# Residual rows scaled and shifted by a norm's vectors 900 instructions behind the norm instead of 400

## The chip, the cores and the metric

The kernel runs on one core of one Trainium2 chip. The metric is the device time of one execution in microseconds (us). A core has five engines with queues of their own: TensorE (PE, with its weight loads shown apart as PEld), VectorE (DVE), ScalarE (ACT), GpSimd (POOL) and SyncE (SP), which here only issues transfers. Each engine takes its instructions strictly in the order in which the program has them; engines wait for each other through semaphores.

## The reference, cut to what matters

One layer of a decoder over 512 tokens of 1024 values: three sublayers, each followed by a layer norm of `ALPHA * h + f(h)`.

```python
def layer_norm(x, g, b):
    mu = jnp.mean(xf, axis=-1, keepdims=True)
    var = jnp.mean(jnp.square(xf - mu), axis=-1, keepdims=True)
    return ((xf - mu) * lax.rsqrt(var + LN_EPS) * g + b).astype(x.dtype)

h = layer_norm(x, ln_in_g, ln_in_b)
f = hybrid_mixer(h, ...)                       # three kinds of attention, one output projection w_out
h = layer_norm(ALPHA * h + f, ln_mix_g, ln_mix_b)
f = mem_attn(h, mem, w_mem_q, w_mem_kv, w_mem_o)
h = layer_norm(ALPHA * h + f, ln_mem_g, ln_mem_b)
f = sq_relu_mlp(h, w_up, b_up, w_down, b_down)
h = layer_norm(ALPHA * h + f, ln_ffn_g, ln_ffn_b)
```

The norm's result is used twice: at once, as the next sublayer's input, and much later, times ALPHA, as the residual that the next sublayer's output is added to.

## The kernel before

Tokens lie in four tiles of 128 rows, `res[0]` to `res[3]` (128 x 1024, float32), which hold the residual. Matrix products run in three passes on a high and a low part of each operand (names `h_...` and `l_...`; `mm3` writes the three). A weight block is loaded by SP (`r_...`), its high part is a cast, its low part a subtraction (`split`).

A norm works like this. The last product of a sublayer (`gemm_tok`, banks `ps_wo` for the mixer and `ps_wmo` for the memory attention) finishes token tile by token tile. For each tile `residual` adds two PSUM banks to `res[t]` and takes statistics (`st_...`, `mv_...`, `ve_...`), all on DVE; POOL computes the reciprocal root (`rs_...`), and `center` on DVE subtracts the mean and multiplies by `rs`. For each pair of tiles TensorE then transposes the centred rows (`ps_lt`); ACT or DVE applies the norm's two vectors along partitions (`h32`), and a cast and a subtraction split it into the next sublayer's operand (`h1T0` to `h1T7` after the mixer, `h2T0` to `h2T7` after the memory attention). With those the next products start: `ps_q` (queries of the memory attention, `w_mem_q`) and `ps_up` (the MLP's first product, `w_up`), first on the columns of tokens 0 to 255, then on the rest.

The residual needs the same scale and shift along rows. `gb_rows` loads the two vectors, broadcast to 128 rows and multiplied by ALPHA (`gbc_mix`, `bbc_mix`, later `gbc_mem`, `bbc_mem`), and `gain_shift` multiplies `res[t]` by the one and adds the other: two operations of 128 x 1024 for each tile, eight for a norm, on DVE or on POOL (`any_tt` leaves the engine open). Their result is read by the adds of the next sublayer's end, over 70 us later for the mixer's norm and some 200 us later for the memory norm.

The order on each engine is not the order of the source. Every instruction is recorded with a due number (`clock`, one more for each instruction), and `issue` lays all of them out with a cost for each: at each step it takes, over all engines, the instruction that can start first by its own clock, among those with equal start the one with the lower due number. It looks no further ahead than 560 due numbers (`LOOK`) beyond the oldest instruction that is not yet placed. `either` instructions go to the engine on which they would end first. `gain_shift` raises the due number of its two instructions by `later`:

```python
def gain_shift(hat, gb, t, later=0.0):
    nc.clock += later
    any_tt(hat[t], hat[t], gb[0], OP.mult)
    any_tt(hat[t], hat[t], gb[1], OP.add)
    nc.clock -= later
```

It is called with `GAIN_LATER` behind the mixer's norm and behind the memory norm. The norm of the input calls it with no delay. At 400 the eight operations lie within the 560 that `issue` looks ahead when their rows are ready.

Of the kernel before, what the change touches and what calls it, by code (L numbers as in the profile page):

```python
# [364 lines left out]
def trunk_kernel(ctx: ExitStack, tc: tile.TileContext, x, mem, ln_in_g, ln_in_b, w_in, gate_w2,  # L365
# [764 lines left out]
# [5 lines that stand above are left out]
# [19 lines left out]
    for t in range(NT):  # L1154
        gain_shift(res, gb, t, GAIN_LATER)

# [51 lines left out]
    for t in range(NT):  # L1208
        gain_shift(res, gb, t, GAIN_LATER)

# [176 lines left out]
GATE_AHEAD = 80.0  # L1387
LOOK = 560.0
KV_STEPS = (0, 0, 0, 1, 3, 3, 2, 4, 1, 1)
GAIN_LATER = 400.0  # L1390
W_SLACK = 300.0
M_SLACK = 600.0
DOWN_LATER = 60.0
# [23 lines left out]
```

## Time and profile before

| | us |
|---|---|
| median of 3 runs | 826.19 (826.02 to 827.07) |
| the profiled execution | 825.4 |
| its span in the trace | 823.6 |
| TensorE busy in the span | 792.5 (96%) |
| DVE busy | 631.3 (77%) |
| ACT busy | 329.2 (40%) |
| POOL busy | 158.2 (19%) |

Times in the trace count from the span's start. Mean granted clock of TensorE over the span is 0.99 of full speed. The mixer's last product ends at 350.0 us, the memory attention runs until 475.8 us, the MLP from there to the end. The two norms concerned therefore lie around 335 to 370 us and 460 to 495 us.

### The profile page before, as it was taken

The page shows a single profiled execution, that of the slowest core. Times are in us where ns is not written, and L with a number is a line of the kernel's source. Part 1 is how long each engine was busy: PE and PEld are TensorE (multiplying, and loading weights), DVE is VectorE, ACT ScalarE, POOL GpSimd, SP SyncE. Part 2 cuts the span into 40 slices and gives each one's busy share as a digit, 9 for nine tenths or more (in the row PEclk, how much of TensorE's full clock was granted, in tenths as well). Part 3 has the DMA queues.
Part 4 walks back from the last instruction along what each step waited for, and adds up shares of the span by engine and source line. Part 5 has one row for each costly group of instructions (what it writes and reads, how often), then busy time and mean ns, then how long its engine had stood idle before and what let it go on. Part 6 is the DMA issues. An engine that isn't in the chain of part 4 may idle for free.

```text
span 823.6 us, 11289 instructions
## 1 busy us (share of the span) xinstructions
PE 792.5 (96%) x4177; PEld 662.8 (80%) x4177; DVE 631.3 (77%) x1111; ACT 329.2 (40%) x634; POOL 158.2 (19%) x173
## 2 busy tenths in 40 slices
PE   7999999999999899989999989999999999899995
PEld 5997769777877888888878889888888888678884
DVE  7737999997649983886553799767777776798778
ACT  4506634577535540233330143333323232585420
POOL 5320142354622210227340210000000000110001
PEclk9999999999999999999999999999999999999998
DMA  8520331603244534023322024645546555467532
GB/s 239 137 53 15 100 94 27 179 9 103 75 152 159 165 120 150 27 77 103 114 92 77 26 77 142 217 154 186 197 137 214 196 174 175 138 219 240 196 126 103
DMA packets 99927, 106.70 MB, mean 130 GB/s; under 512 B 10448, under 2 KB 79136, under 8 KB 99872
## 3 DMA queue, kind: packets, MB, share of 16 engines
q1 hardware_dynamic: 97344, 99.00, 38.1%
q10 hardware_dynamic: 2528, 6.98, 2.5%
q8 instruction: 33, 0.54, 0.3%
q14 instruction: 22, 0.18, 0.1%
HBM read 94.69 MB, written 10.49 MB: 128 GB/s over the span
## 4 chain that ended last, share of the span: by engine, by line
PE 68%; DVE 16%; issue 2%; ACT 1%; DMA 1%; POOL 0%; DVEq 0%; ACTq 0%; POOLq 0%
PE ps_up L356 20%; PE ps_dn L356 17%; PE ps_wmo L356 4%; PE ps_wo L356 4%; PE ps_q L356 3%; DVE res L356 2%; PE ps_km L356 2%; PE ps_z L356 2%; DVE acc L356 2%; PE ps_vm L356 2%; PE ps_gg L356 1%; PE ps_dq L356 1%; PE ps_mo L356 1%; DVE m L356 1%; DVE s L356 1%
## 5 line engine op out<-in xcount | busy, mean ns | idle before, releaser
L356 PE MATMUL ps_up<-h2T,h_up 128*128 128x512 f32 (+1 forms) x576 | 161.1, 366 | 0.0
L356 PEld LDWEIGHTS ps_up<-h2T,h_up 128*128 128x128 f32 x576 | 104.0, 189 | 17.6 <-DVE h2T L356 0.2
L356 PE MATMUL ps_up<-h2T,l_up 128*128 128x512 f32 (+1 forms) x288 | 104.8, 366 | 0.5 <-DVE l_up L356 0.5
L356 ACT ACTIVATE ur<-ps_up,gb_all 128x512 f32<-128x512 f32 x32 | 22.1, 690 | 108.7 <-PE ps_up L356 108.7
L356 PEld LDWEIGHTS ps_up<-h2T,l_up 128*128 128x128 f32 x288 | 54.1, 189 | 9.5 <-DVE l_up L356 0.7
L356 PE MATMUL ps_dn<-h_dn,a 128*128 128x512 f32 x192 | 59.3, 389 | 0.0
L356 DVE TENSOR_TENSOR l_dn<-r_dn,h_dn 128x1024 fp32r<-128x1024 f32 (+1 forms) x44 | 45.2, 1026 | 5.1 <-ACT h_dn L356 3.7
L356 PE MATMUL ps_dn<-h_dn,ends 128*128 128x512 f32 x128 | 47.7, 396 | 0.7 <-DVE ends L356 0.7
L356 POOL TENSOR_TENSOR a<-keep,a 128x1024 fp32r<-128x1024 f32 x1 | 4.1, 4067 | 228.3 <-PE ps_dn L356 228.3
L356 PE MATMUL ps_q<-h1T,h_wmq 128*128 128x256 f32 (+1 forms) x192 | 45.7, 329 | 0.0
L356 ACT ACTIVATE h<-ps_lt,gb_all 128x256 f32<-128x256 f32 x20 | 10.2, 566 | 85.6 <-PE ps_lt L356 84.8
L356 PEld LDWEIGHTS ps_dn<-h_dn,a 128*128 128x128 f32 x192 | 36.0, 188 | 7.5
L356 PE MATMUL ps_wmo<-h_wmo,oT 128*128 128x512 f32 x128 | 40.7, 393 | 0.0
L356 DVE TENSOR_TENSOR l_up<-r_up,h_up 128x1024 fp32r<-128x1024 f32 x32 | 38.9, 1220 | 2.2 <-ACT h_up L356 0.5
L356 PE MATMUL ps_wo<-h_wo,mix 128*128 128x512 f32 x128 | 40.3, 392 | 0.0
L356 PE MATMUL ps_dn<-l_dn,a 128*128 128x512 f32 x96 | 37.3, 389 | 0.0
L356 PEld LDWEIGHTS ps_q<-h1T,h_wmq 128*128 128x128 f32 x192 | 32.9, 197 | 2.5 <-DVE h1T L356 0.2
L356 PE MATMUL ps_q<-h1T,l_wmq 128*128 128x256 f32 (+1 forms) x96 | 31.3, 330 | 0.5 <-DVE ve_mix L356 0.5
L356 DVE TENSOR_SCALAR h_up<-r_up 128x1024 fp32r<-128x1024 f32 x17 | 11.8, 692 | 26.1 <-PE ps_up L356 22.6
L356 PEld LDWEIGHTS ps_dn<-h_dn,ends 128*128 128x128 f32 x128 | 24.5, 192 | 6.3 <-DVE ends L356 1.2
L356 PEld LDWEIGHTS ps_wo<-h_wo,mix 128*128 128x128 f32 x128 | 24.0, 188 | 4.9
L356 PEld LDWEIGHTS ps_wmo<-h_wmo,oT 128*128 128x128 f32 x128 | 24.0, 188 | 4.8
(408 smaller groups left out, 2095.6 us busy)
## 6 DMA issues: line engine op xcount, KB each, us to landing
r_dn<-in_w_down_dram SPq DMA_DIRECT2D x48, 512.0 KB, 4.3
r_up<-in_w_up_dram SPq DMA_DIRECT2D x32, 512.0 KB, 4.5
r_t<-t SPq DMA_DIRECT2D x16, 512.0 KB, 3.6
r_kvv<-in_w_mem_kv_dram SPq DMA_DIRECT2D x8, 512.0 KB, 4.0
r_kvk<-in_w_mem_kv_dram SPq DMA_DIRECT2D x8, 512.0 KB, 3.6
r_wo<-in_w_out_dram SPq DMA_DIRECT2D x8, 512.0 KB, 4.4
r_wmq<-in_w_mem_q_dram SPq DMA_DIRECT2D x8, 512.0 KB, 5.0
r_wmo<-in_w_mem_o_dram SPq DMA_DIRECT2D x8, 512.0 KB, 3.4
```

The source lines that it names most:

```text
L356: f(*[real(a) for a in args], **{k: real(a) for k, a in kwargs.items()})
```

## The change

One number: the residual's scale and shift is due 900 instructions behind the norm, not 400.

```diff
-GAIN_LATER = 400.0
+GAIN_LATER = 900.0
```

Since 900 is more than the 560 that `issue` looks ahead, the sixteen operations can only be placed once the oldest unplaced instruction is 340 numbers past the norm. What comes of it on the engines is seen in three places.

DVE behind the mixer's norm, from the second half of token tile 2. Before (`res0` is scaled and shifted between the statistics of tiles 2 and 3):

```order
L356 TENSOR_TENSOR res2_2615<-ps_wo1_3375,res2_2615 128x512
L356 TENSOR_TENSOR res0_2608<-res0_2608,gbc_mix_3223 128x1024
L356 BN_STATS st_mix_3594<-res2_2615 128x6
L356 TENSOR_TENSOR res3_2625<-ps_wo0_3383,res3_2625 128x512
L356 BN_AGGR mv_mix_3680<-st_mix_3594 128x2
L356 BN_STATS st_mix_3683<-res3_2625 128x6
L356 TENSOR_TENSOR res3_2625<-ps_wo1_3387,res3_2625 128x512
L356 TENSOR_SCALAR ve_mix_3696<-mv_mix_3680 128x1
L356 TENSOR_TENSOR res0_2608<-res0_2608,bbc_mix_3253 128x1024
L356 BN_STATS st_mix_3683<-res3_2625 128x6
L356 TENSOR_SCALAR res2_2615<-res2_2615,mv_mix_3680,rs_mix_3709 128x1024
```

Now:

```order
L356 TENSOR_TENSOR res2_2615<-ps_wo1_3375,res2_2615 128x512
L356 BN_STATS st_mix_3594<-res2_2615 128x6
L356 TENSOR_TENSOR res3_2625<-ps_wo0_3383,res3_2625 128x512
L356 BN_AGGR mv_mix_3674<-st_mix_3594 128x2
L356 BN_STATS st_mix_3676<-res3_2625 128x6
L356 TENSOR_SCALAR ve_mix_3681<-mv_mix_3674 128x1
L356 TENSOR_SCALAR res2_2615<-res2_2615,mv_mix_3674,rs_mix_3684 128x1024
L356 TENSOR_TENSOR res3_2625<-ps_wo1_3387,res3_2625 128x512
```

Both operations of `res0` are gone from here, and the centring of `res2` stands ahead of the second add of `res3` and its statistics. The memory norm's rows read the same with `ps_wmo`, `gbc_mem` and `h2T`. The eight operations of the mixer's norm now stand together on DVE behind the softmax of the memory attention's second head, four of them between the two query tiles (`qT`) of the third head; those of the memory norm stand on DVE in the MLP's fourth pair of `up` blocks. POOL, which had one or two of each eight, has none.

TensorE behind the mixer's last product. Before, 24 products of the first query tile stand ahead of these rows, and the transposes of tile 2 follow three half-begun tiles:

```order
L356 MATMUL ps_q_3687<-h1T7_3654,l_wmq_3498 128x256
L356 MATMUL ps_q_3726<-h1T0_3610,h_wmq_3718 128x256 x2
L356 MATMUL ps_q_3729<-h1T0_3610,h_wmq_3720 128x256 x2
L356 MATMUL ps_q_3734<-h1T0_3610,h_wmq_3722 128x256 x2
L356 MATMUL ps_lt_3739<-ident_88,res2_2615 128x128
L356 MATMUL ps_lt_3741<-ident_88,res2_2615 128x128
L356 MATMUL ps_lt_3743<-ident_88,res2_2615 128x128
L356 MATMUL ps_lt_3745<-ident_88,res2_2615 128x128
L356 MATMUL ps_q_3726<-h1T0_3610,l_wmq_3736 128x256
```

Now:

```order
L356 MATMUL ps_wo1_3387<-h_wo_3456,mix7_2299 128x512
L356 MATMUL ps_q_3694<-h1T0_3610,h_wmq_3492 128x256 x2
L356 MATMUL ps_q_3694<-h1T0_3610,l_wmq_3498 128x256
L356 MATMUL ps_q_3694<-h1T1_3618,h_wmq_3492 128x256 x2
L356 MATMUL ps_q_3694<-h1T1_3618,l_wmq_3498 128x256
L356 MATMUL ps_lt_3704<-ident_88,res2_2615 128x128
L356 MATMUL ps_lt_3706<-ident_88,res2_2615 128x128
L356 MATMUL ps_lt_3708<-ident_88,res2_2615 128x128
L356 MATMUL ps_lt_3712<-ident_88,res2_2615 128x128
L356 MATMUL ps_q_3694<-h1T2_3625,h_wmq_3492 128x256 x2
```

The transposes of tile 2 came behind 30 products of the queries and now come behind 6. Those of tile 3 came behind 60 and now come behind 54. In the MLP's start the same holds with 30 and 6, 59 and 52.

POOL around the memory norm. Before:

```order
L356 TENSOR_TENSOR h2T0_4779<-h32_4767,h2T0_4779 128x256
L356 TENSOR_TENSOR res1_2613<-res1_2613,gbc_mem_4229 128x1024
L356 TENSOR_TENSOR rs_mem_4878<-ve_mem_4865,mhalf_84 128x1
L356 TENSOR_TENSOR rs_mem_4928<-ve_mem_4916,mhalf_84 128x1
L356 TENSOR_SCALAR h2T4_4803<-h32_4994 128x256
```

Now:

```order
L356 TENSOR_TENSOR h2T0_4779<-h32_4767,h2T0_4779 128x256
L356 TENSOR_TENSOR rs_mem_4853<-ve_mem_4850,mhalf_84 128x1
L356 TENSOR_TENSOR l_up_4871<-r_up_4654,h_up_4858 128x1024
L356 TENSOR_TENSOR rs_mem_4915<-ve_mem_4900,mhalf_84 128x1
L356 TENSOR_SCALAR h2T1_4787<-h32_4950 128x256
L356 TENSOR_SCALAR h2T0_4779<-h32_4948 128x256
```

The scaling of `res1` is gone, and the low part of one `w_up` block, DVE's before, stands on POOL between the roots of tiles 2 and 3. The casts of `h2T0` and `h2T1` for the second half of the tokens are POOL's now, and DVE's before; after the mixer's norm that is so too, but there no weight block comes to POOL.

## Rows read from the trace of the kernel before

**Rows 1.** The page's first line: span and instructions.
```profile
span 823.6 us, 11289 instructions
```
**Rows 2.** Waits of PE, 340 to 440 and 440 to 530: total us, times, longest.
```profile
PE ps_mpt L356 <- DVE mp L356: 1.7, 2, 1.2
PE ps_ms L356 <- DVE qT L356: 0.6, 1, 0.6
...
PE ps_lt L356 <- DVE mv_mem L356: 1.9, 1, 1.9
```
**Rows 3.** Timeline of PE, mixer's norm: start, us, instruction, count [idle before <-releaser].
```profile
349.81 0.39 PE L356 MATMUL ps_wo<-h_wo,mix 128*128 128x512 f32 x1
...
355.71 0.63 PE L356 MATMUL ps_lt<-ident,res 128*128 128x128 f32 x4 [1.92 <-DVE mv_mix L356]
...
362.00 1.47 PE L356 MATMUL ps_lt<-ident,res 128*128 128x128 f32 x12
```
**Rows 4.** Stretches: us, busy (count) of PE, PEld, DVE, ACT, POOL; clock, DMA, GB/s.
```profile
357.50:361.00 3.50, 3.50 (x19) 3.50 (x18) 3.46 (x4) 0.00 (x0) 0.88 (x1) 0.53 0.85 238
...
482.00:486.00 4.00, 3.52 (x30) 3.50 (x30) 4.00 (x6) 0.00 (x0) 1.46 (x1) 1.00 0.59 161
```
**Rows 5.** Timeline of DVE, mixer's norm.
```profile
339.21 0.15 DVE L356 TENSOR_SCALAR ve_mix<-mv_mix 128x1 f32<-128x1 f32 x1
340.09 0.81 DVE L356 TENSOR_SCALAR res<-res,mv_mix,rs_mix 128x1024 f32<-128x1024 f32 x1 [0.73 <-POOL rs_mix L356]
...
344.23 4.57 DVE L356 TENSOR_TENSOR h1T<-h,h1T 128x256 fp32r<-128x256 f32 x7
...
349.33 1.21 DVE L356 TENSOR_TENSOR res<-res,gbc_mix 128x1024 f32<-128x1024 f32 x1
350.46 0.68 DVE L356 BATCH_NORM_STATS2 st_mix<-res 128x6 f32<-128x512 f32 x1
...
353.03 1.22 DVE L356 TENSOR_TENSOR res<-res,bbc_mix 128x1024 f32<-128x1024 f32 x1
...
354.76 0.80 DVE L356 TENSOR_SCALAR res<-res,mv_mix,rs_mix 128x1024 f32<-128x1024 f32 x1
...
356.75 2.35 DVE L356 TENSOR_TENSOR l_wmq<-r_wmq,h_wmq 128x1024 fp32r<-128x1024 f32 x2
...
364.05 1.42 DVE L356 TENSOR_TENSOR h1T<-h,h1T 128x256 fp32r<-128x256 f32 x4
```
**Rows 6.** Timeline of POOL, mixer's norm.
```profile
344.10 2.42 POOL L356 TENSOR_TENSOR res<-res,gbc_mix 128x1024 f32<-128x1024 f32 x1
353.19 1.46 POOL L356 TENSOR_TENSOR rs_mix<-ve_mix,mhalf 128x1 f32<-128x1 f32 x1 [6.67 <-DVE ve_mix L356]
```
**Rows 7.** Timeline of PE, memory norm.
```profile
475.55 0.39 PE L356 MATMUL ps_wmo<-h_wmo,oT 128*128 128x512 f32 x1
...
481.39 0.63 PE L356 MATMUL ps_lt<-ident,res 128*128 128x128 f32 x4 [1.87 <-DVE mv_mem L356]
...
486.19 1.47 PE L356 MATMUL ps_lt<-ident,res 128*128 128x128 f32 x12
```
**Rows 8.** Timeline of ACT, memory norm.
```profile
474.25 2.94 ACT L356 CAST h_up<-r_up 128x1024 fp32r<-128x1024 f32 x3 [2.86 <-PE ps_wmo L356]
```
**Rows 9.** Timeline of POOL, memory attention's third head.
```profile
404.02 1.05 POOL L356 TENSOR_SCALAR gbc_mem<-gbc_mem 128x1024 f32<-128x1024 f32 x1 [12.90 <-DMA gbc_mem<-in_ln_mem_g_dram]
...
406.45 2.40 POOL L356 TENSOR_TENSOR bbc_mem<-bbc_mem,bd 128x1024 f32<-128x1024 f32 x1 [0.17 <-DMA bd<-in_b_down_dram]
```
**Rows 10.** Timeline of DVE, memory attention's third head.
```profile
405.73 0.69 DVE L356 SCALAR_TENSOR_TENSOR qT<-ps_q,qT 128x512 fp32r<-128x512 f32 x1 [4.75 <-ACT qT L356]
406.66 3.27 DVE L356 TENSOR_TENSOR l_wmo<-r_wmo,h_wmo 128x1024 fp32r<-128x1024 f32 x1 [0.24 <-ACT h_wmo L356]
```
**Rows 11.** Timeline of DVE, then of PE, MLP.
```profile
521.33 0.42 DVE L356 TENSOR_TENSOR mid<-s,mid 128x256 fp32r<-128x256 f32 x1
...
530.16 0.39 PE L356 MATMUL ps_dn<-h_dn,mid 128*128 128x512 f32 x1
```

## The prediction

> **What bounds the kernel now.** I read the waits of TensorE first, then its timeline around the two norms, then DVE and POOL at the same instants, last the granted clock. TensorE is busy for nearly the whole span [rows 1], so time is won only where it stands still or runs slowly. In the two norms that the change touches it stands still for 1.9 us each in front of the transposes of token tile 2 [rows 3, 7]; the second is in the table of waits too [rows 2]. Behind the first stop it is granted 0.53 of its clock for 3.5 us: 19 products there, against 30 in 3.52 us of work at full clock, where one takes 0.12 us [rows 4]. So that stretch loses 3.5 - 19 x 0.12 = 1.2 us to the lower of the two levels (1.2 against 2.4 GHz). The second stop, as long, is followed by full clock.
>
> Why it stops: DVE. While POOL scales `res1` (344.10 to 346.52), seven subtractions of `h1T` on DVE take 4.57 us, 0.65 each; four of the same kind take 1.42, 0.355 each, where POOL is quiet [rows 5, 6]. Seven at 0.355 would be 2.5, so POOL's one operation cost DVE 2.1 us: the two do not run side by side. Then DVE itself scales and shifts `res0` (starts 349.33 and 353.03, next instruction 1.13 later), and the second of these holds up POOL's root: 1.46 us, ended at 354.65, while from variance to centring an undisturbed tile needs 0.88 in all (339.21 to 340.09) [rows 5, 6]. Only then can `res2` be centred, at 354.76, and transposed 0.95 later [rows 3, 5]. All three delays are the operations that the change moves.
>
> **The change, part by part.** Times are on the clock of the profiled execution before.
>
> *Mixer's norm.* Without POOL's operation the seven subtractions end at 344.23 + 2.5 = 346.7 instead of 348.8. From there to the end of the variance it was 353.03 - 348.8 = 4.2 us; less 1.13 for the scaling, and less 0.6 for the second add of `res3`, which now stands behind the centring, that is 2.5, so 349.2 [rows 5]. With 0.88 from variance to centring, counted from a start some 0.05 earlier, `res2` is centred from 350.1 and transposed from 351.05. TensorE ends the mixer's product at 350.03 (0.22 behind the start of its last instruction [rows 3]) and has six products now, 0.7 us: it arrives at 350.75 and waits 0.3 us. For `res3` DVE has left: the rest of the centring and the add 1.3, three subtractions of weights at 1.17 [rows 5], statistics 0.8, root 0.85: centring at 356.6, transposes at 357.5. TensorE needs 0.4 for four transposes and 48 x 0.12 = 5.8 for products and arrives at 357.25. So those transposes start at 357.5 and not at 362.00 [rows 3], behind 54 products and not 60: 4.5 - 0.7 = **3.8 us won**; the 1.2 us of low clock are in it, since a wait of 0.3 should not bring it on. What is late next is the second half of `h1T`: its first two casts go from DVE to POOL, one behind the other. A piece of 256 columns takes DVE 0.355 [rows 5], so two are about 0.7 us, an estimate for POOL too, which may be slower; some of that lies beside the products of the first half. I take 0.4 off. The scaling and shifting that stood in front of the queries' split is gone too, and TensorE waited 0.6 us in front of the first head's scores (`ps_ms`) and 1.7 - 1.2 = 0.5 in front of its softmax (`ps_mpt`) [rows 2]; I give back 0.6 of this 1.1. Sum for this norm: **4.0 us**, bounds 1.8 (the seven subtractions do not shorten) and 4.8.
>
> *Memory norm.* The work repeats 475.55 - 349.81 = 125.74 us later [rows 3, 7], so `res2` could be centred from 475.85. But POOL now has the subtraction for a `w_up` block directly behind the root. Its cast on ACT starts at 474.25 and one of three takes 0.98 [rows 8], so its subtraction could start at 475.3, before the root ends; such a subtraction of 1024 columns takes POOL 2.4 us [rows 6, 9]. Both the centring (held by the root's semaphore) and POOL's next instruction (held by nothing) become ready at the same instant, and POOL's has no semaphore to wait for. I take POOL as first: centring from 478.2, transposes from 479.15, TensorE waits 2.65 us instead of 1.87. The transposes of `res3` come 0.4 + 46 x 0.12 later, at 485.05 and not at 486.19 [rows 7], behind 52 products and not 59: 1.1 - 0.8 = +0.3, less 0.4 for the casts as above: **0**. If DVE is first, it is 479.15 - 476.8 = 2.35 better: **+2.3**. No row of the trace has the two within 0.1 us, so both ends stay.
>
> *Here the Trainium skill bears on it.* The page SBUF — State Buffer, section Who interferes with whom, says that VectorE and GpSimd share one pair of ports, that the instruction issued first holds it to its end, and that the other is blocked fully; it counts VectorE's operations with two inputs in SBUF among those that want it, and single-input ones in the two-port mode. The trace agrees: 2.1 us lost by DVE to an operation of 2.42 [rows 5, 6]. By that rule the order of issue decides the memory norm: 0 or +2.3, and nothing between.
>
> *Where the operations go.* The mixer's eight now run on DVE in the second and third head, at 1.13 each 9.0 us. DVE was idle for 4.75 us between the third head's query tiles [rows 10], into which four of them go (4.5); there POOL prepares the memory vectors, two operations of 1.05 and one of 2.40 [rows 9]. Before, that last one blocked DVE's weight subtraction (3.27 instead of 1.17) [rows 9, 10], and TensorE waited 1.2, the longer of the two `ps_mpt` stops, in front of the softmax [rows 2]. Now both sides are pushed into each other, but POOL's 2.40 no longer stands in front of everything. I put the change there at **0**, bounds -1.9 (four operations and POOL's three, 9.0 us, against 4.75 idle and 2.4 us of score products already in hand) and +0.7. The memory norm's eight go into the MLP's fourth pair, 9.0 us. DVE had `mid` ready 8.4 us ahead of its product there (521.75 to 530.16) [rows 11], idle time comes on top, so I put that at 0; uncovered it would be 0.6.
>
> **Sum.** 4.0 + 0 + 0 + 0 = 4.0 us off 825.4, the profiled execution, so 821.4. The median before is 826.19, 0.8 above it; against the median the same gain gives **822.2 us**. A measurement of this kernel can tell about 0.2%, 1.65 us, from no change.
>
> **The rivals.**
>
> *DVE first at the memory norm.* For it: the centring is a short way from the semaphore, 0.03 us behind the root's end. Against it: POOL's next instruction waits for nothing. It gives 2.3 more: 819.9.
>
> *Low clock behind the memory norm's stop.* The stop grows to 2.65, and one of the two stops before was followed by 3.5 us at 0.53 [rows 4]. Price 1.2: 823.4. The page TensorE: Matmul & The Clock Gate, section What's actually happening, says that the monitor's window runs freely and is not set by the kernel; the trace agrees, since of two equal stops one brought the low level. By that rule the same program could show either.
>
> *The gain is given back in the heads.* The four operations and POOL's three collide, TensorE waits 1.9 more for the third head's scores and runs slowly behind that (1.2), and the memory norm's stop brings the low clock too (1.2): 4.0 - 4.3, so 826.5, no change. For it: DVE was nearly full at such places. Against it: 4.75 us of idle time.
>
> *The early transposes make it slower.* TensorE's order is fixed, and the transposes of `res2` stand 24 products (2.9 us) earlier. If the seven subtractions keep their 4.57 us at both norms (something other than POOL stretched them), all that follows is 2.1 later: the mixer's norm wins 1.9 less 1.2 for the clock, so 0.7, and the memory norm, with POOL first, stops for 4.7 us and loses 2.1, and 1.2 to the clock behind it. In all 2.6 lost, and with the third head at its bound 4.5: 828.8 to 830.7; I name **829.0**. It decides from the point at which DVE's way to the centring is shortened by less than about 2.5 us. Against it: 0.65 against 0.355 us for the same instruction, exactly while POOL works.
>
> **How the numbers follow.** Forecast 822.2 (0.40), DVE first 819.9 (0.23), low clock 823.4 (0.17), no change 826.5 (0.13), slower 829.0 (0.07). The range reaches from 818.8, the DVE-first case with the upper bound of the mixer's norm and some of the third head's, to 825.2, the low-clock case with the mixer's norm nearer to its lower bound: that leaves out the last two cases. Faster by over 0.2%: the first three, 0.80. Within 0.2%: 0.13. Slower: 0.07.
>
> **What would show it.** On DVE seven subtractions of `h1T` in about 2.5 us, on TensorE a wait under 0.6 in front of the first transposes behind `ps_wo`, full clock from 350 to 365, and transposes of tile 3 some 7.5 us behind the end of `ps_wo`, not 12. Behind `ps_wmo`: a wait of about 2.6 (POOL first) or 0.3 (DVE first), to be read from who starts first behind `rs_mem`. It is wrong if the seven subtractions still take over 4 us, if TensorE waits over 2 us more inside the memory attention than before, or if a wait for `l_dn`, `mid` or `l_up` appears between 515 and 560.

## The result, and the profile after

| | before | changed |
|---|---|---|
| median of the runs | 826.39 us (826.02 to 827.07) | 822.29 us (820.61 to 822.55) |
| ratio, 95% interval | 1 | 0.9946 (0.993 to 0.9962) |
| the profiled execution | 825.4 us | 822.55 us |

The change makes the kernel faster by 4.1 us in the medians and by 2.85 us between the two profiled executions. Stretches of low clock can make such a difference between two executions; what of it the traces show stands below, under the changed kernel again and in the part on the prediction.

To see where the time went I cut the span at four instants that every kernel here has: the first product of the queries (`ps_q`), the first of `w_mem_o` (`ps_wmo`), the first of `w_up` (`ps_up`) and the first of the MLP's second matrix (`ps_dn`). Each stretch holds the same 460, 228 and 256 instructions of TensorE in all kernels, in whatever order, so its length shows all that TensorE lost in it. Times are in us, from TensorE's timeline of each profiled execution.

| kernel | `ps_q` to `ps_wmo` (mixer's norm, heads) | `ps_wmo` to `ps_up` | `ps_up` to `ps_dn` (memory norm) |
|---|---|---|---|
| before | 76.73 | 49.01 | 38.75 |
| changed | 72.46 | 49.09 | 40.00 |
| e10_again (changed) | 72.42 | 49.08 | 38.51 |
| e1_mix_only | 72.42 | 49.04 | 40.26 |
| e2_mem_only | 76.20 | 49.07 | 40.04 |
| e3_low_on_dve | 72.44 | 49.03 | 36.56 |
| e4_no_pool_scale | 72.65 | 49.02 | 36.69 |
| e5_no_dve_scale | 72.97 | 49.04 | 36.78 |
| e6_one_back | 76.11 | 49.08 | 38.53 |
| e7_late_mix | 71.11 | 49.09 | 36.52 |
| e8_casts | 72.07 | 49.06 | 36.87 |
| e9_dve_only | 78.78 | 49.10 | 37.72 |

The change wins 4.27 us in the first stretch and loses 1.25 in the third, where its profiled execution ran partly at low clock. The rest of the MLP costs nothing: from the first to the last pair's `ps_dn` it took 194.48 us before (514.52 to 709.00) and 194.47 after (511.75 to 706.22).

**The mixer's norm.** DVE's timeline of the changed kernel (start, us, instruction, count, idle time before and what ended it), which answers to [rows 5]:

```profile
344.41 2.42 DVE L356 TENSOR_TENSOR h1T<-h,h1T 128x256 fp32r<-128x256 f32 x7
...
349.40 0.14 DVE L356 TENSOR_SCALAR ve_mix<-mv_mix 128x1 f32<-128x1 f32 x1
350.20 0.81 DVE L356 TENSOR_SCALAR res<-res,mv_mix,rs_mix 128x1024 f32<-128x1024 f32 x1 [0.67 <-POOL rs_mix L356]
```

and TensorE's, which answers to [rows 3]:

```profile
349.98 0.39 PE L356 MATMUL ps_wo<-h_wo,mix 128*128 128x512 f32 x1
...
351.16 0.63 PE L356 MATMUL ps_lt<-ident,res 128*128 128x128 f32 x4
...
357.38 1.47 PE L356 MATMUL ps_lt<-ident,res 128*128 128x128 f32 x12
...
360.03 0.62 PE L356 MATMUL ps_q<-h1T,h_wmq 128*128 128x256 f32 x3 [0.35 <-POOL h1T L356]
```

The seven subtractions take 2.42 us, not 4.57. `res2` is centred 4.56 earlier than before, the transposes of tile 2 carry no idle time in brackets, and those of tile 3 start at 357.38, not at 362.00. What is late next are the casts that came to POOL: a stop of 0.35. The granted clock is full here, in contrast to [rows 4] (stretch, us, busy time and count of PE, PEld, DVE, ACT and POOL, clock, DMA share, GB/s):

```profile
352.00:356.00 4.00, 4.00 (x36) 4.00 (x35) 3.74 (x6) 0.00 (x0) 0.18 (x1) 1.00 0.47 142
356.00:360.00 4.00, 3.68 (x32) 3.48 (x31) 2.25 (x5) 2.03 (x5) 1.16 (x3) 1.00 0.79 235
...
476.00:480.00 4.00, 4.00 (x23) 4.00 (x23) 3.23 (x5) 0.00 (x0) 1.49 (x1) 0.57 0.72 223
```

The last row lies behind the memory norm's stop and is low: 23 instructions of TensorE in 4 us.

**The memory norm.** POOL, then DVE, then TensorE, which answer to [rows 7]:

```profile
471.06 0.55 POOL L356 TENSOR_TENSOR rs_mem<-ve_mem,mhalf 128x1 f32<-128x1 f32 x1 [5.29 <-DVE ve_mem L356]
471.58 2.37 POOL L356 TENSOR_TENSOR l_up<-r_up,h_up 128x1024 fp32r<-128x1024 f32 x1
```

```profile
471.65 2.85 DVE L356 TENSOR_SCALAR res<-res,mv_mem,rs_mem 128x1024 f32<-128x1024 f32 x1 [0.67 <-POOL rs_mem L356]
```

```profile
474.64 0.63 PE L356 MATMUL ps_lt<-ident,res 128*128 128x128 f32 x4 [2.03 <-DVE res L356]
...
482.11 1.47 PE L356 MATMUL ps_lt<-ident,res 128*128 128x128 f32 x12
...
484.77 0.50 PE L356 MATMUL ps_up<-h2T,h_up 128*128 128x256 f32 x2 [0.35 <-POOL h2T L356]
```

POOL starts its subtraction 0.07 us ahead of DVE's centring. The centring's record begins at once but lasts 2.85 us, where it takes 0.81 in the mixer's norm: the time in which it is held shows as busy time of DVE, not as idle time. TensorE waits 2.03.

**The third head.** Four of the moved operations meet POOL's preparation of the memory vectors here. DVE, POOL and TensorE, which answer to [rows 9, 10]:

```profile
398.95 4.05 DVE L356 TENSOR_TENSOR res<-res,bbc_mix 128x1024 f32<-128x1024 f32 x2
```

```profile
400.08 1.85 POOL L356 TENSOR_SCALAR bbc_mem<-bbc_mem 128x1024 f32<-128x1024 f32 x1
402.01 3.22 POOL L356 TENSOR_TENSOR bbc_mem<-bbc_mem,bd 128x1024 f32<-128x1024 f32 x1
```

```profile
403.65 0.75 PE L356 MATMUL ps_ms<-kms,qT 128*128 128x256 f32 x4 [1.21 <-DVE qT L356]
...
409.91 0.96 PE L356 MATMUL ps_mpt<-ident,mp 128*128 128x128 f32 x6 [0.75 <-DVE mp L356]
```

Both engines are held: DVE's two additions take 2.0 each instead of 1.13, POOL's two operations 1.85 and 3.22 instead of 1.05 and 2.40 for such operations. TensorE's stops in this head are 1.96 together, against 1.23 before.

### The profile page after: what moved, and what is told of

It is laid out like the page before. It is cut to its first block, busy times and chain, and to the rows that moved or that the text cites. A ratio compares the mean times of both kernels' runs of the same rounds, so it can differ in the third digit from the quotient of the medians.

```text
span 820.8 us, 11293 instructions
## 1 busy us (share of the span) xinstructions
PE 790.4 (96%) x4177; PEld 662.5 (81%) x4177; DVE 636.3 (78%) x1118; ACT 328.0 (40%) x631; POOL 144.5 (18%) x169
## 4 chain that ended last, share of the span: by engine, by line
PE 69%; DVE 16%; issue 3%; ACT 1%; POOL 1%; DVEq 0%; ACTq 0%; POOLq 0%
PE ps_up L356 21%; PE ps_dn L356 18%; PE ps_wo L356 5%; PE ps_wmo L356 4%; PE ps_q L356 4%; DVE acc L356 2%; DVE m L356 2%; PE ps_km L356 2%; DVE res L356 2%; PE ps_z L356 2%; PE ps_vm L356 2%; PE ps_dq L356 1%; DVE s L356 1%; PE ps_mo L356 1%; PE ps_ms L356 1%
## 5 line engine op out<-in xcount | busy, mean ns | idle before, releaser
L356 PE MATMUL ps_up<-h2T,h_up 128*128 128x512 f32 (+1 forms) x576 | 163.1, 368 | 0.4 <-POOL h2T L356 0.4
```

Of the source, the lines that this page charges most:

```text
L356: f(*[real(a) for a in args], **{k: real(a) for k, a in kwargs.items()})
```

## The experiments

Theory: POOL's operations hold DVE's and DVE's hold POOL's, and DVE's own operations stand in front of the centring; taking them away shortens the way to the transposes, and the memory norm does not gain because POOL's subtraction for `w_up` takes the place of the operation that was removed. Main rivals: the gain comes from both norms or from the new order of TensorE, and the delay itself counts. All ratios are to the kernel before, run in the same series.

**One norm at a time.** The edit is in the two calls of `gain_shift`; here the memory norm's:

```diff
-        gain_shift(res, gb, t, GAIN_LATER)
+        gain_shift(res, gb, t, 400.0)
```

> The mixer's norm at 900, the memory norm left at 400. Theory (the gain comes from the mixer's norm alone, and the memory norm gave some of it back because POOL's subtraction for a w_up block held DVE's centring): the last ps_wmo product comes some 4.0 us earlier than in the kernel before, the memory norm reads as before (stop 1.87 us), and the time is 821 to 822.3, not above the changed kernel. Rival (both norms bring about half): 824.3.

Measured 822.35 us, ratio 0.9959 (0.9947 to 0.9972), against 0.9946 for the whole change in its own series. The first stretch is that of the changed kernel (72.42). Behind the memory norm TensorE stops as before:

```profile
476.88 0.63 PE L356 MATMUL ps_lt<-ident,res 128*128 128x128 f32 x4 [1.86 <-DVE mv_mem L356]
```

The third stretch, at 40.26, is 1.5 longer than before all the same: here the clock fell behind this stop (0.86 and 0.71 from 476 to 484), as it did not in the profile of before.

> The memory norm at 900, the mixer's norm left at 400. Theory: nothing is won, since DVE's centring of tile 2 meets POOL's subtraction as in the changed kernel (centring 2.85 us, stop of TensorE about 2.0): 826.4 to 827.7. Rival (both norms bring about half): 824.3. If the planner's order puts no such subtraction on POOL here: stop under 0.6 and 824.0, which would speak for the theory too.

Measured 825.31 us, ratio 1.0001 (0.9992 to 1.001): nothing won. (The times that I had named were counted from the 826.39 of the first series; the kernel before ran at 825.46 in this one.) The collision is there to the hundredth, POOL first and then DVE:

```profile
475.31 2.37 POOL L356 TENSOR_TENSOR l_up<-r_up,h_up 128x1024 fp32r<-128x1024 f32 x1
```

```profile
475.38 2.85 DVE L356 TENSOR_SCALAR res<-res,mv_mem,rs_mem 128x1024 f32<-128x1024 f32 x1 [0.67 <-POOL rs_mem L356]
```

So the mixer's norm brings all of the gain that can be told from noise.

**POOL's subtraction taken away.** The order stays as the planner laid it out; one instruction (`i`, the `l_up` on POOL) goes to DVE, behind the variance of tile 3:

```diff
 ...
+    behind = [j for j in order[order.index(i):] if ops[j].took == "vector"]
+    ops[i].took = "vector"
+    line.remove(i)
+    line.insert(line.index(behind[2]) + 1, i)
```

> The changed kernel, with one instruction moved: the subtraction for the w_up block (l_up) that stood on POOL between the roots of tiles 2 and 3 stands on DVE, behind the variance of tile 3. Theory: the centring of res2 takes 0.8 instead of 2.85 us, TensorE's stop in front of the transposes of tile 2 falls from 2.03 to under 0.4, and the low clock behind it goes: 820.0 without the clock, 818.8 with it. Rival (the centring was slow for another reason, or the time is lost again in front of the transposes of tile 3 because DVE has 1.17 us more ahead of them): 822 to 823.

Measured 819.83 us, ratio 0.9928 (0.9914 to 0.9941). DVE's centring and the transposes:

```profile
472.19 0.81 DVE L356 TENSOR_SCALAR res<-res,mv_mem,rs_mem 128x1024 f32<-128x1024 f32 x1 [0.66 <-POOL rs_mem L356]
```

```profile
473.15 0.63 PE L356 MATMUL ps_lt<-ident,res 128*128 128x128 f32 x4
```

The centring takes 0.81 us, no stop is left, and the third stretch falls to 36.56: 1.95 below e10_again, which has full clock there, and 3.44 below the changed kernel's profile, which has not. The 1.17 us more on DVE ahead of tile 3 cost nothing. So POOL's subtraction is what kept the memory norm from gaining.

**One operation put back.** The reverse test on the changed kernel: one of the sixteen (`i`, `res1` times `gbc_mix`) goes back to POOL, behind POOL's part of `h1T0` (`h`) and the last transposes that read `res1` (`last`).

```diff
 ...
+    line.remove(i)
 ...
+    line.insert(max(h, last) + 1, i)
+    ops[i].took = "gpsimd"
```

> The changed kernel, with one of the sixteen operations put back: the scaling of res1 behind the mixer's norm runs on POOL behind its part of h1T0, as in the kernel before; all else stands as changed. Theory (POOL's operation holds DVE): the subtractions of h1T take 4.5 us again instead of 2.42, TensorE stops for about 2.2 us in front of the transposes of tile 2 behind 6 products, and the time is 2.1 above the changed kernel, 824.4, or 825.6 with a stretch of low clock behind the stop; up to 0.7 less where the third head gets easier by one operation. Rival (POOL's operation is harmless and the gain comes from the order of the transposes and from DVE's own operations): subtractions in 2.4 us, 822.3.

Measured 824.76 us, ratio 0.9986 (0.9977 to 0.9995): nearly the whole gain is gone with one operation. POOL, DVE and TensorE:

```profile
344.30 2.39 POOL L356 TENSOR_TENSOR res<-res,gbc_mix 128x1024 f32<-128x1024 f32 x1
```

```profile
344.43 4.56 DVE L356 TENSOR_TENSOR h1T<-h,h1T 128x256 fp32r<-128x256 f32 x7
...
352.35 0.81 DVE L356 TENSOR_SCALAR res<-res,mv_mix,rs_mix 128x1024 f32<-128x1024 f32 x1 [0.66 <-POOL rs_mix L356]
```

```profile
353.31 0.90 PE L356 MATMUL ps_lt<-ident,res 128*128 128x128 f32 x4 [2.21 <-DVE res L356]
```

The subtractions take 4.56 us again and TensorE stops for 2.21, this time behind 6 products, with low clock behind it (0.69 from 352 to 356, 0.88 from 356 to 360). The first stretch is 3.65 longer than in the changed kernel, 2.2 of it the stop. The early transposes alone bring nothing: with POOL's operation in its place they come too early, behind 6 products.

**Each cause left out alone, in the order of before.** In both kernels the instructions are dropped when they are written out; nothing else moves.

```diff
+    out = {i for later, t, i in prog.gains if later and t == 1 and ops[i].took in ("gpsimd",)}
+    return [i for i in order if i not in out]
```

This is the first of the two; the second has `t == 0` and `"vector"`.

> The kernel before in its own order, with one operation of each norm left out: POOL's scaling of res1 (by gbc_mix and by gbc_mem), so res1 is not scaled. Theory (POOL's operation holds DVE): the seven subtractions take 2.4 and not 4.57 us, res2 is centred 2.1 earlier, and TensorE's stops in front of tile 2's transposes (1.92 and 1.87) and behind them (0.49 and 0.48) go, without any change of order: 820.7, or 819.5 where the low clock behind the mixer's stop goes too. Rival (the order of TensorE's transposes brings the gain): 825.4.

Measured 819.54 us, ratio 0.9924 (0.991 to 0.9938).

```profile
344.31 2.43 DVE L356 TENSOR_TENSOR h1T<-h,h1T 128x256 fp32r<-128x256 f32 x7
```

> The kernel before in its own order, with DVE's two operations on res0 left out in each norm (scaling and shift, so res0 keeps its centred values); POOL's scaling of res1 stays. Theory: the subtractions stay at 4.57 us, but the variance of tile 2 comes 1.13 earlier and its root takes 0.55 and not 1.46, so res2 is centred 2.0 earlier and the two stops go here too: 820.7, or 819.5 with the clock. So each of the two causes alone would be enough to remove a stop of 1.9. Rival (only POOL's operation counts): stops of 1.5 or more stay, 824.5.

Measured 819.83 us, ratio 0.9927 (0.9914 to 0.9939). DVE, POOL and TensorE:

```profile
344.37 4.56 DVE L356 TENSOR_TENSOR h1T<-h,h1T 128x256 fp32r<-128x256 f32 x7
...
352.90 0.81 DVE L356 TENSOR_SCALAR res<-res,mv_mix,rs_mix 128x1024 f32<-128x1024 f32 x1
```

```profile
352.31 0.55 POOL L356 TENSOR_TENSOR rs_mix<-ve_mix,mhalf 128x1 f32<-128x1 f32 x1 [5.68 <-DVE ve_mix L356]
```

```profile
353.86 0.63 PE L356 MATMUL ps_lt<-ident,res 128*128 128x128 f32 x4
```

In both the stop in front of tile 2's transposes is gone in both norms; the one of 0.5 behind it stays, which my expectation had wrong. Since the stop was 1.92 and each cause is worth about 2, removing either one alone is enough in this order, with 24 more products ahead of the transposes. In the order of the change it is not: in e6_one_back DVE's own operations are gone too and `res2` is centred 0.55 earlier than here (352.35 against 352.90), yet TensorE stops for 2.21, since only 6 products stand ahead. So the early transposes need POOL's operation gone as well; whether they need DVE's own gone too no run tells. The first stretch is 72.65 and 72.97 against 72.46 with the change, but its parts differ (here the stops of the first head stay, there the third head loses), so the difference is no measure of the second cause.

**Bound to DVE, with the delay left at 400.**

```diff
-        any_tt(hat[t], hat[t], gb[0], OP.mult)
-        any_tt(hat[t], hat[t], gb[1], OP.add)
+        f = nc.vector.tensor_tensor if later else lambda *a, op: any_tt(*a, op)
+        f(hat[t], hat[t], gb[0], op=OP.mult); f(hat[t], hat[t], gb[1], op=OP.add)
```

> The kernel before with the delay at 400 as it was, but the sixteen operations bound to DVE instead of left open to POOL. Theory (it is POOL's one operation against DVE's subtractions that counts, not the delay): the subtractions take 2.4 us behind the mixer's norm, the stop of 1.92 goes although four or five of the eight operations still stand among the norm's own; behind the memory norm POOL again has a w_up subtraction behind the root of tile 2, but 30 products stand ahead of tile 2's transposes there, so its stop is under 0.6: 820.0, or up to 821.5. Rival (the delay is what counts): 824 or more.

Measured 825.76 us, ratio 0.9996 (0.9987 to 1.0005): a miss. The mixer's norm did what the theory said (the subtractions take 2.43 and the stop is gone). But the planner now puts two weight subtractions of the first head on POOL and four of the operations in front of its softmax on DVE. DVE, POOL and TensorE there:

```profile
376.32 4.85 DVE L356 TENSOR_SCALAR mp<-mp,mst 128x256 f32<-128x256 f32 x3
```

```profile
376.04 4.72 POOL L356 TENSOR_TENSOR l_wmq<-r_wmq,h_wmq 128x1024 fp32r<-128x1024 f32 x2
```

```profile
376.36 0.41 PE L356 MATMUL ps_mpt<-ident,mp 128*128 128x128 f32 x2 [0.56 <-DVE mst L356]
378.71 0.41 PE L356 MATMUL ps_mpt<-ident,mp 128*128 128x128 f32 x2 [1.70 <-DVE mp L356]
381.06 0.66 PE L356 MATMUL ps_mpt<-ident,mp 128*128 128x128 f32 x2 [1.94 <-DVE mp L356]
```

Three multiplications of the softmax take 4.85 us between POOL's two; four take 1.90 in the third head of the changed kernel. The stops come to 4.2 us, and the clock falls behind them (0.53 and 0.61 from 380 to 388). The expectation missed in the memory norm too: POOL's subtraction holds the centring there again, and TensorE stops for 1.50 where under 0.6 was expected, in spite of the products ahead.

```profile
479.30 2.38 POOL L356 TENSOR_TENSOR l_up<-r_up,h_up 128x1024 fp32r<-128x1024 f32 x1
```

```profile
479.81 2.42 DVE L356 TENSOR_SCALAR res<-res,mv_mem,rs_mem 128x1024 f32<-128x1024 f32 x1
```

```profile
482.38 0.63 PE L356 MATMUL ps_lt<-ident,res 128*128 128x128 f32 x4 [1.50 <-DVE res L356]
```

So the delay does count, for the place at which the sixteen operations, and the work that they push to POOL, come to lie.

**The changed kernel again.**

> The changed kernel once more, on the chip of the last runs. Theory: the same rows up to hundredths (subtractions 2.42, stop 0.3 or less in the mixer's norm, centring 2.85 and a stop of 2.0 behind the memory norm); behind that stop the granted clock is low or full from one execution to the next, so the time is 822.3 where it is low and 820.7 where it is full. Rival (the low clock belongs to the kernel): low in every profile, and no execution under 821.5.

Measured 821.13 us (820.96 to 822.43), ratio 0.9951 (0.9937 to 0.9964). The stop behind the memory norm is 2.02, as in the first profile, and the clock behind it is full:

```profile
476.00:480.00 4.00, 4.00 (x36) 4.00 (x35) 3.17 (x5) 0.00 (x0) 1.49 (x1) 1.00 0.73 226
```

36 instructions in these 4 us, against 23. The third stretch is 38.51 and not 40.00: 1.5 us for the same program, with the same stops and another clock. The rival (low in every profile) falls. That all slow executions of this kernel owe their time to this is not shown: only the profiled ones have a trace, and the one of 822.43 us had the same mean clock, 0.991, as those of 821.0 and 821.1.

**A better version.** Two kernels try what the runs pointed to: the mixer's operations in a place where POOL has little to do, and POOL's casts elsewhere. The first edit is in the mixer's call; beside it all sixteen are bound to DVE as in e9_dve_only, and `l_up` is moved as in e3_low_on_dve.

```diff
-        gain_shift(res, gb, t, GAIN_LATER)
+        gain_shift(res, gb, t, 1200.0)
```

> The changed kernel with the w_up subtraction on DVE, as in e3_low_on_dve, and the eight operations of the mixer's norm due 1200 instructions behind it instead of 900, all sixteen on DVE: those of the mixer's norm come to lie in the last product of the memory attention. Theory: the third head loses the collision of DVE's four operations with POOL's three, its stops fall from 2.0 us together to about 1.2 (the kernel before), and nothing new stops: 0.8 less than e3_low_on_dve, 819.0. Rival (they delay the low parts of w_mem_o and TensorE waits in ps_wmo): 820 or more.

Measured 818.31 us (817.43 to 819.36), ratio 0.9909 (0.9895 to 0.9923). One stop is left between the mixer's norm and `ps_wmo` besides the 0.34 behind the casts:

```profile
407.74 0.96 PE L356 MATMUL ps_mpt<-ident,mp 128*128 128x128 f32 x6 [0.89 <-DVE mp L356]
```

The eight operations lie between 429 and 441 us, beside the product of `w_mem_o`, at 1.1 to 1.3 us each, and `ps_wmo` to `ps_up` keeps its 49.09. This is the lowest median of the study; by the intervals it is not told apart from e3_low_on_dve (0.9914 to 0.9941), and the gain over it is read from the first stretch, 71.11 against 72.44.

```diff
-                split(hT[kt][:, 0, cols], hT[kt][:, 1, cols], h32)
+                (split_off if hT is not first_hT[0] else split)(hT[kt][:, 0, cols], hT[kt][:, 1, cols], h32)
```

`split_off` is `split` without POOL for the cast; `first_hT` is the input norm's operand.

> e7_late_mix, and the high-part casts of h1T and h2T kept off POOL (on ACT or DVE). Theory: the two stops of 0.34 us in front of the second half's products, behind POOL's casts, go: 0.7 less than e7_late_mix, 818.3. Rival (ACT and DVE have them no sooner, or the order of the subtractions moves the centring back): the same time or more.

Measured 818.6 us, ratio 0.9913 (0.9899 to 0.9926): not better, the rival's case. The two stops are still 0.33 and 0.32, now behind DVE's part, and the third head's stop is 1.35 instead of 0.89.

## Why the prediction was right, point by point

822.2 us was forecast and 822.29 measured. The agreement to 0.1 us is closer than the argument was; its terms were off by up to 0.7 us and in part cancel, and the changed kernel's profiled execution has a stretch of low clock that the sum left out. So the last digit is luck.

*What bounds it.* Right. DVE's way to the centring was the cause of both stops, POOL's one operation cost it 2.1 (4.57 to 2.42, and back to 4.56 in e6_one_back), and DVE's own operations about as much (e5_no_dve_scale). What I had not seen is that in the order of before the removal of either alone suffices, and that in the order of the change it does not: e6_one_back stops for 2.21 with DVE's own operations gone.

*Mixer's norm: 4.0 forecast.* The transposes of tile 3 came 357.38 - 350.20 = 7.18 behind the first `ps_q` product instead of 362.00 - 350.03 = 11.97. That is 4.79, less the six products that now follow them (0.7): 4.07 for a term of 3.8. The casts on POOL cost 0.35 for a term of 0.4. In the first head both stops went, 0.62 + 0.42 = 1.04, where I gave back 0.6; they stay in e2_mem_only, e4_no_pool_scale and e5_no_dve_scale, and no run tells which of the operations there they hang on.

*Third head: 0 forecast, bounds -1.9 and +0.7.* It lost 1.96 - 1.23 = 0.73. The mechanism was named, but I put it at 0 although the middle of my own bounds was a loss of 0.6. This is the term that was most off. In the run of e10_again the two stops were 0.36 and 1.60, the same sum in another split. The four terms make 4.07 - 0.35 + 1.04 - 0.73 = 4.03; the stretch as a whole shows 4.27, so 0.24 is not assigned.

*Memory norm: POOL first, 0.* Right: POOL was first in the traces of the changed kernel, of its second run and of e2_mem_only. With full clock the stretch won 38.75 - 38.51 = 0.24. The stop was 2.03 and not 2.65: POOL's subtraction ended at 473.95, and the held centring needed only 0.55 behind that, not the 0.81 of a whole one; that is 0.26 of the 0.62, the rest is spread over POOL's start and TensorE's arrival. The trace of before has 60 products ahead of tile 3's transposes in this norm, not 59, which takes 0.1 off the sum. The rival "DVE first" fell; what it was worth is shown by e3_low_on_dve, 1.95 for a price of 2.3.

*Low clock behind the memory norm's stop.* This rival came true in the profiled execution and not in e10_again. It cost 1.49 for a price of 1.2. On the scale of the profiled executions the forecast was 821.4 without it and 822.6 with it; measured were 821.05 and 822.55. The medians agree so well because two things that the change did not make nearly cancel: three of the changed kernel's four runs lie at 822.1 to 822.6, one of them the profiled execution with low clock, and the profiled execution of before lies 1.0 under the median of before, 826.39, and under each of its four runs. Why those took longer no trace shows. Between the profiled executions without low clock behind this stop the gain is 825.4 - 821.05 = 4.35, for a forecast of 4.0.

*The clock, by the page.* The Trainium skill, TensorE: Matmul & The Clock Gate, section What's actually happening, says that the window runs freely. The traces agree: of stops of 2.02 to 2.06 behind the memory norm, the one of 2.03 and the one of 2.06 (e2_mem_only) were followed by low clock, those of 2.02 (e10_again) and 2.05 (e6_one_back) by full clock.

*The two other rivals.* "Given back in the heads" did not come, but e9_dve_only shows its mechanism at full price: 4.2 us of stops and low clock behind. "The early transposes make it slower" did not come either; e6_one_back puts POOL's operation back and shows its first half, a stop of 2.21 and a loss of 3.65 with the clock, for a price of 2.1 and 1.2. Against before the first stretch still wins 0.62 there, where this rival had 0.7.

*Where the operations go, MLP.* Right: 194.48 and 194.47 us.

## What to carry to other kernels

An instruction with spare time is not free on an idle engine: one operation of POOL took 2.1 us from DVE and, through it, 1.9 from an engine that was 96% busy. When such work is moved, look at what the scheduler puts in the gap that it leaves (here a weight subtraction on POOL that cost the second norm its 2 us), and read the length of single instructions against the same one elsewhere, since being held shows as busy time. And compare stretches that hold the same work, because times of whole executions mix in the clock: here 1.5 us for one and the same program.

## What the runs showed that I had not expected

A centring, one tensor and two scalars per row, is held by POOL like an operation with two tensors: 2.85 us against 0.81, and the softmax's multiplications of 256 columns likewise (three in 4.85). An operation that reads a PSUM bank was not: in the third head of the changed kernel a query tile's low part, which took 0.69 in [rows 10], ran inside POOL's addition from 402.01 to 405.23. DVE's timeline there:

```profile
402.92 0.68 DVE L356 SCALAR_TENSOR_TENSOR qT<-ps_q,qT 128x512 fp32r<-128x512 f32 x1
403.52 2.79 DVE L356 TENSOR_TENSOR l_wmo<-r_wmo,h_wmo 128x1024 fp32r<-128x1024 f32 x1
```

The next one, with two tensors in SBUF, was held until POOL had ended (2.79, where one of this size takes 1.2). The Trainium skill, SBUF — State Buffer, section Who interferes with whom, has both: DVE with one input in SBUF does not contend unless it runs in a two-port mode, and an operation of a tensor with scalars can enter one. The traces agree in what was held (2.85) and what was not (0.68); in which mode an instruction ran they do not show.

The reciprocal root on POOL, 128 x 1, takes 0.55 to 0.56 us alone in these two norms, and 0.55 beside DVE's statistics, but 1.41 to 1.49 where DVE runs a subtraction or a shift of 1024 columns beside it; so the holding goes both ways, for so small an instruction too.
